# One hybrid decoder layer in f32: w_o's weight sums moved to DRAM, the first pair's norms and rotation placed earlier, the next two pairs' rotation and a table placed later

## The chip, the cores and the metric

The kernel runs on one core of a Trainium2 chip. The metric is the device time of one execution in microseconds (us), lower is better; a time is the median of several executions. The engines that matter are TensorE (PE: matmuls and transposes), VectorE (DVE), ScalarE (ACT), GpSimd (POOL, which here issues some DMAs and raises small vectors to the power -1/2) and the DMA queues that SyncE (SP) and POOL issue. Each engine works through its own list of instructions in order, and an instruction waits until what it reads is there.

## What is computed

One layer on 512 rows of width 2048. The reference, cut to what matters:

```python
h = rms_norm(x, g_mix); z = h @ w_in                       # 2048 -> 7168 columns
aq, ak, av, rq, rk, rv, rg = jnp.split(z, split_at, axis=-1)
aq = rotate(rms_norm_per_head(aq, q_norm)); ak = rotate(rms_norm_per_head(ak, k_norm))
a_out = moba_attention(aq, ak, av)                         # 8 heads of 128, 512 keys, causal
r = retention_chunkwise(rotate(rq), rotate(rk) / sqrt(128), rv)   # 8 heads
r_out = silu(rg) * (rms_norm_per_head(r) * g_ret)
x = x + concat(a_out, r_out) @ w_o                         # 2048 x 2048
h2 = rms_norm(x, g_ffn)
x = x + (silu(h2 @ w_gate) * (h2 @ w_up)) @ w_down         # width 5632
x = x + (p @ w_ple_proj) * sigmoid(rms_norm(x, g_ple) @ w_ple_gate + b)
```

With 512 keys and blocks of 256 the block selection always takes the one past block, so the attention is plain causal attention.

## The kernel before, in words

**Products.** Every f32 product is made of three fast ones. `split` makes of a value a high part (ACT, line 54, `wh` for weights) and a low part (DVE, line 55, `wl` = raw minus `wh`); `mm3` then runs three matmuls on PE (line 63). A weight tile `raw` (128 x 1024, 512 KB) is loaded by SP, split by ACT and DVE, and used by PE. The big projections ("groups") go further: a seven-product scheme (products named 1, 5, 6, 3, 7, 2, 4) needs sums and differences of quarters of the weight matrix. These are either added by DVE on the fly (line 81, `raw<-raw`), or were added ahead in DRAM by transfers that accumulate: `summed` lists such transfers, `move` (line 157) lets POOL issue the next one behind a given ACT instruction (`lead`). Before the change this is done for three parts of w_gate/w_up, w_down and w_ple_gate.

**Stages.** From 0 to about 364 us the first stage runs: the first pair's q and k projection, then four groups (values, pairs, values, gates) driven by `run`, which steps a counter `i` and calls `beside(i)` for loads and other side work. From about 364 to about 740 us the mix runs: for i = 0 to 3 the attention of the pairs of heads, for i = 4 to 7 the retention. A projection of the following pair is cut into pieces, one piece per "slot"; `tick()` counts the slots, and `at_slot(n, fn)` and the tables ATTEND, RETAIN, V_AT and MIXED say at which slot a piece of the attention is written between the matmuls of the projection. So PE always has projection matmuls around an attention piece, and the order of PE's instructions is fixed by the code (`keep_in_program_order`). The order on DVE, ACT, POOL and SP is chosen by a scheduler from the code's order, the dependencies and hints such as `tc.issue_after`. After the mix come w_o (two groups, n = 0 and 1), the gated layer and the last gate until the end.

**The attention of a pair, for each of four blocks of 128 rows** (b = 0 to 3): `load_block` loads z from DRAM (`zr<-z`, SP) where an earlier stage has stored it; `in_place` rotates it on DVE (lines 833, 831, 81: `m<-zr,rope` x2, `zr<-zr,rope`, `zr<-zr,m`), ACT scales it by its norms; PE transposes it (`tp<-ident,zr`), ACT and DVE split it (`qkH`, `qkL`); PE makes scores (`at<-qkL,qkH`), DVE adds the mask, takes the maximum and scales it (lines 913, 915, 917), ACT takes the exponential (`pt`), DVE divides by the sum (lines 921, 922), PE transposes the weights (`tp<-ident,pt`), they are split into PH and PL, and PE multiplies them with the values v. The blocks of the first pair (i = 0) are loaded and rotated at the end of the first stage, their norms made there from squares on ACT and sums on DVE (line 845); the norms of pairs i = 1 and 2 were made in the first stage (`pairs`); pair i = 3 is rotated straight out of its projection. The rotation tables `rope` are built from `cs` and `sn` at the end of the first stage (lines 775 and 778), the retention's table `ropeT` is scaled at slot 32 with PE transposing `rstd` for it. `p_tiles` hands out PH and PL, and a part of each is zeroed once (line 930).

Of the kernel before, what the change touches and what calls it, by code (L numbers as in the profile page):

```python
# [10 lines left out]
F32 = mybir.dt.float32  # L11
F32R = mybir.dt.float32r
# [21 lines left out]
def layer_kernel(ctx, tc, x, xT, pT, g_mix, wqk, w_vg, qk_norm, g_ret, w_ow, g_ffn,  # L34
# [133 lines left out]
    def run(before=lambda i: None, behind=False):  # L168


        i = -3
        parts = {}
        while i < len(steps) or due:
            now[0] = i
            before(i)
            for n, act in ((2, "extract"), (3, "add"), (0, "multiply")):
                if 0 <= i + n < len(steps):
                    g, p, u = steps[i + n]
                    made = getattr(g, act)(p, u)
# [409 lines left out]
    def values(i):  # L589
# [7 lines left out]
                    vd[i][:, tb, k, nh * T:(nh + 1) * T].bitcast(F32), t.bitcast(F32)))  # L597
        return evacuate(finish)

    def pairs():  # L600
        def finish(th, nh, b, part, _):
            tb = 2 * th + b
            t = part
            if (th, nh) == (0, 0):
                t = ev_tile("o", 4, name="zq")
                nc.scalar.activation(t, part, AF.Copy)
            later(1, lambda: nc.sync.dma_start(zd[1 + nh][tb], t))
            sq = ev_tile("o", 4, name="sq")
            ms = stat.tile([P, 4], F32, name=f"ms{nh}_{tb}", bufs=1)
            for j in range(4):  # L610
                c = slice(j * HD, (j + 1) * HD)
                nc.scalar.activation(sq[:, c], t[:, c], AF.Square, accum_out=ms[:, j:j + 1])
            nc.vector.tensor_scalar(ms, ms, 1.0 / HD, eps1[:, tb:tb + 1], op0=ALU.mult, op1=ALU.add)
            power(ms, ms, 4)
            known[1 + nh][tb] = ms
        return evacuate(finish)

    def gates():
# [12 lines left out]
    def beside(i):  # L631

        if i == 3:
            for t, c in ((ident, ident_c), (gf, g_ffn), (gp, g_ple), (gr, g_ret)):
                nc.sync.dma_start(t, c)
        if -2 <= i < NC // 2 - 2:
            if i == -2:
                first.load(0)
            else:
                first.load(i + 2)  # L640
            chunks[i + 2] = []
            for k in (2 * i + 4, 2 * i + 5):
                if i == -2:
                    first.start(k)
                chunks[i + 2].append(h_chunk(k))
        if 0 <= i - 1 < NC // 2:
            first_factors(i - 1, chunks.pop(i - 1))
        for at, q in ((3, "11"), (7, "12"), (11, "22")):
            if at <= i < at + 4:
                groups[0].load(q, i - at)  # L650
        if 8 <= i < 24:
            b, s = divmod(i - 8, NS)
            t = ev_tile("o", 4, name="xn")
            tc.keep_in_program_order(nc.sync.dma_start(t, x[b * P:(b + 1) * P, s * T:(s + 1) * T]))
            nc.scalar.activation(t, t, AF.Square, accum_out=ssq[0][:, b, s:s + 1])
        elif i == 24:
            rstd_of(ssq[0], rstd[0])

            nc.vector.tensor_tensor(eps1, rstd[0], rstd[0], op=ALU.mult)
            nc.vector.reciprocal(eps1, eps1)  # L660
            nc.vector.tensor_scalar(eps1, eps1, EPS, None, op0=ALU.mult)
        if i >= 56 and i % 4 == 0 and i < 112:
            move(gu_moves.pop(0), lead[0])

    run(beside)
    s_ctx.close()
# [36 lines left out]
    stream = [wqk[i, u] for i in range(1, NPAIR + 2) for u in range(NC // 2)] + [pT] + [w_pp[n] for n in range(NS)]  # L703
    ready = []
    fetched = []

    def fetch(behind=None):
        raw = rawq.tile([P, 2, T], F32, name="raw", tag=tags.pop(0))
# [6 lines left out]
    def weights():  # L715
        while fetched + stream and len(ready) < (3 if len(stream) > NS - 1 else 2):
            if not fetched:
                fetch()
            raw = fetched.pop(0)
            wh = wq.tile([P, 2, T], F32R, name="wh", tag="wh")  # L720
            wl = wq.tile([P, 2, T], F32R, name="wl", tag="wl")
            made = split(wh, wl, raw)
            lead[0] = made[0]
            ready.append((wh, wl))
            if gu_moves and slot[0] > 18 and len(stream) % 2:
                move(gu_moves.pop(0), made[0])
        return ready.pop(0)

    def raw_pair():
# [29 lines left out]
    tab = []  # L759
    tabs = [ap.tile([P, 2, NB, HD], F32, name="rope", tag=tag) for tag in ("rope", "rope2")]  # L760
    cs, sn = (ap.tile([P, NB, HD], F32, name=n, tag="pt", bufs=2) for n in ("cs", "sn"))
    nc.sync.dma_start(cs, rope_c[:, 0])
# [8 lines left out]
        return ins  # L771

    blocks = {}
    for s in range(2):
        nc.vector.tensor_tensor(tabs[0][:, s], cs, gain[:, s:s + 1, :].to_broadcast([P, NB, HD]), op=ALU.mult)
        for u in range(2):
            here, there = slice(u * 64, u * 64 + 64), slice(64 - u * 64, 128 - u * 64)
            nc.vector.tensor_tensor(tabs[1][:, s, :, here], sn[:, :, here],
                                    gain[:, s:s + 1, there].to_broadcast([P, NB, 64]), op=ALU.mult)
    rstd1 = rstd[0]  # L780
    last_load = [load_block(0, b) for b in range(NB)][-1]
    for _ in range(4):
# [2 lines left out]
    def load_ropeT():  # L785
        t = ap.tile([P, 2, T], F32, name="ropeT", tag="rope")
        nc.sync.dma_start(t, ropeT_c)
        bc = ev_tile("A", name="bc")
        nc.scalar.activation(bc, over_partitions(rstd1), AF.Copy)
        nc.vector.tensor_tensor(t, t, bc[:, None, :].to_broadcast([P, 2, T]), op=ALU.mult)  # L790
        tab.append(t)

    def qk_pair():
        H = ap.tile([P, T], F32R, name="qkH", tag="qkH", bufs=4)
        L = far.tile([P, T], F32R, name="qkL", tag="qkL", bufs=4)
        return H, L

    def v_of(i):
        v = ap.tile([P, NB, 2, 256], F32R, name="v", tag="v")
        j = i % NPAIR  # L800
        for b in range(NB):
            nc.sync.dma_start(v[:, b].bitcast(F32), vd[i // NPAIR][:, b, :, j * 256:(j + 1) * 256].bitcast(F32))
        return v
# [4 lines left out]
        PL = far.tile([P, 1664], F32R, name="PL", tag="PL")  # L808
        return PH, PL

    kept_p = []

    def weighted(v, ps, j):

# [42 lines left out]

    def in_place(i, b, made, norms):
        of = blocks[i][b]
        sq = squares(of) if i == 0 else None  # L860
        m = rm_tile("m", (P, 2, 2, 2, HD // 2))
        z = of.rearrange("p (s h d) -> p s h d", s=2, h=2)
        whole, *halves = turn(z, m, of, b)
        for step in halves + [whole]:
            step()
        norms.append(norm(b, sq) if i == 0 else known[i][b])
        made.append(rotated(z, m, norms[b]))

    def qk_attn(i):

        made, norms = [], []
        if i == 0:
            for b in range(NB):
                in_place(0, b, made, norms)
        elif i < NPAIR - 1:
            for b in range(NB):
                n = (5, 17)[i - 1] + 2 * b
                at_slot(n, lambda b=b: load_block(i, b, lead[0]))
                at_slot(n + 3, lambda b=b: in_place(i, b, made, norms))
        else:  # L880
# [13 lines left out]
    def attend(z, norms, v, j):  # L894
# [29 lines left out]

        def weights_turned(qb):
            if not ps:
                if not kept_p:
                    kept_p.extend(p_tiles())
                    for t in kept_p:
                        nc.vector.tensor_scalar(t[:, 1408:1536], ident, 0.0, None, op0=ALU.mult)  # L930
                ps.extend(kept_p)
            PH, PL = ps
            nk = (qb + 1) * P
# [20 lines left out]
    def qk_ret(i):  # L954

        made = []
        accs = projection(False)
        both = raw_pair()
        half = HD // 2
        cs, sn = tab[0][:, 0, :], tab[0][:, 1, :]  # L960
# [83 lines left out]
    def mixed(i, made):  # L1044
        spilled = spill(s_mix, i, 0, (lambda shape: rm_tile("o", shape, F32R)) if i < 2 * NPAIR - 2 else None)
        direct = into(s_o, i)
        assert (not s_o) == (i < 2 * NPAIR - 2)
        factors(*made, lambda p: (direct if p in s_o else spilled)(p))

    four = lambda n, m=None: (n, n + 1, *((n + 4, n + 5) if m is None else (m, m + 1)))  # L1050
    V_AT = (3, 27, 54, 80, 100, 119, 144, 162)
# [3 lines left out]
              ((73, four(77), four(81), 89), (83, four(87), four(91), 99)))  # L1055
    RETAIN = (((100, 100, 103, 109, 116), (108, 110, 111, 117, 123)),
# [3 lines left out]
    MIXED = (28, 56, 81, 104, 126, 151, 171, 191)  # L1060

    def heads(i, made):

# [26 lines left out]

    for i in range(2 * NPAIR):
        if i == NPAIR:
            load_ropeT()
        qk = qk_attn(i) if i < NPAIR else qk_ret(i)
        heads(i, qk)
    assert not gu_moves
    h_ctx.close()
    pools["s"] = ctx.enter_context(pool("s2"))
    s_o.update({p: Factors(p) for p in "1563"})
# [52 lines left out]
    for n in range(2):  # L1152
# [4 lines left out]
                            reload(s_c, s_h2, 4, behind | {"1": 4}) if n else lambda p: None))  # L1157

    def swiglu(j):
        kg = min(j // 4, 2)  # L1160
# [207 lines left out]
```

## Time and profile before

| | us |
|---|---|
| median of 3 executions | 2336.1 (2335.06 to 2339.81) |
| the profiled execution, its own time | 2336.76 |
| span of the profiled execution (first to last recorded work) | 2335.0 |
| PE busy within the span | 2296.6 |
| DVE busy | 1926.5 |
| ACT busy | 1229.3 |
| POOL busy | 117.2 |
| moved by DMA | 519.72 MB |

Times in rows of the trace are counted from the start of the span. A row of the timeline has the start, the duration, the engine, the line, the operation, output and inputs, and in brackets the idle time of the engine before it and what released it. A row of the windows has, for each engine, its busy time in the window and the number of its instructions, then the clock that was granted to PE (1.00 is full), the mean busy share of the 16 DMA engines, and GB/s. A row of the waits has the engine and what it was about to do, the engine and the result it waited for, the us in total, how often, and the longest.

### The profile page before, as it was taken

What the parts mean: (1) busy time and instruction counts of PE and PEld (TensorE: products, weight loads), DVE (VectorE), ACT (ScalarE), POOL (GpSimd) and SP (SyncE); (2) the same over time, 40 slices, a digit from 0 to 9 for tenths busy, and PEclk for the clock granted to TensorE, in tenths of its full rate; (3) what the DMA queues carried; (4) which work ended last, traced back from release to release, by engine and by line L of the source; (5) the groups of instructions that cost most, each with busy time, mean ns of one, the idle gap of its engine ahead of it and who ended that gap; (6) DMA issues with size and microseconds to landing.
All of it is one profiled execution on the core that took longest, in us unless ns stands there. A gap on an engine that the chain in (4) does not pass through costs nothing.

```text
span 2335.0 us, 29426 instructions
## 1 busy us (share of the span) xinstructions
PE 2296.6 (98%) x10445; PEld 1891.6 (81%) x10445; DVE 1926.5 (83%) x2601; ACT 1229.3 (53%) x1882; POOL 117.2 (5%) x135
## 2 busy tenths in 40 slices
PE   9999998999999999999999999999999999999999
PEld 7888877788887887888888888888888878888877
DVE  8887777877777987888988898889888877788798
ACT  8646444555565566545554555455445443447643
POOL 0004010100111000000000000000000000000000
PEclk9999999999999999999999999999999999999999
DMA  6635854557686789467556754775596776869863
GB/s 240 233 133 174 268 181 142 167 148 221 188 286 234 285 299 355 139 217 251 160 152 221 251 155 154 224 242 152 188 382 206 253 289 202 295 230 359 293 207 126
DMA packets 183843, 519.72 MB, mean 223 GB/s; under 512 B 20240, under 2 KB 33168, under 8 KB 179600
## 3 DMA queue, kind: packets, MB, share of 16 engines
q1 hardware_dynamic: 169600, 467.50, 56.2%
q0 software_dynamic: 13952, 50.34, 10.1%
q8 instruction: 82, 1.34, 0.2%
q14 instruction: 65, 0.53, 0.1%
q10 hardware_dynamic: 144, 0.01, 0.0%
HBM read 413.95 MB, written 149.95 MB: 242 GB/s over the span
## 4 chain that ended last, share of the span: by engine, by line
PE 53%; DVE 5%; DMA 3%; issue 1%; ACT 1%; SPq 0%; ACTq 0%; DVEq 0%
PE Y L63 23%; PE Z L63 15%; PE X L63 14%; DMA raw<-in_w_dn 2%; DVE wl L55 2%; DVE raw L81 2%; PE tp L68 1%; ACT wh L54 1%; DMA raw<-in_w_gu 0%; DMA pp<-pp 0%; DMA xin<-x 0%; DVE o L55 0%; DVE e L81 0%; DVE t L78 0%; DVE e L1273 0%
## 5 line engine op out<-in xcount | busy, mean ns | idle before, releaser
L54 ACT ACTIVATE wh<-raw 128x1024 fp32r<-128x1024 f32 (+1 forms) x740 | 782.8, 1059 | 867.2 <-PE Y L63 309.5
L55 DVE TENSOR_TENSOR wl<-raw,wh 128x1024 fp32r<-128x1024 f32 (+1 forms) x740 | 902.2, 1222 | 281.9 <-ACT wh L54 280.5
L63 PE MATMUL Y<-wh,s 128*128 128x512 f32 (+1 forms) x1704 | 537.5, 389 | 1.0 <-ACT wh L54 1.0
L81 DVE TENSOR_TENSOR raw<-raw 128x1024 f32<-128x1024 f32 x348 | 420.9, 1223 | 27.9 <-DMA raw<-in_w_vg 11.2
L63 PE MATMUL Z<-wh,s 128*128 128x512 f32 x1212 | 382.3, 389 | 0.2 <-ACT wh L54 0.2
L63 PEld LDWEIGHTS Y<-wh,s 128*128 128x128 f32 x1704 | 319.3, 188 | 66.6 <-ACT wh L54 1.4
L63 PE MATMUL Y<-wl,s 128*128 128x512 f32 x852 | 333.2, 391 | 0.8 <-DVE wl L55 0.4
L63 PE MATMUL X<-wh,s 128*128 128x512 f32 x1008 | 319.2, 390 | 3.8 <-ACT wh L54 2.1
L63 PEld LDWEIGHTS Z<-wh,s 128*128 128x128 f32 x1212 | 227.0, 188 | 46.6 <-ACT wh L54 0.7
L63 PE MATMUL Z<-wl,s 128*128 128x512 f32 (+1 forms) x606 | 238.5, 394 | 2.4 <-DVE wl L55 2.3
L63 PEld LDWEIGHTS X<-wh,s 128*128 128x128 f32 x1008 | 189.1, 188 | 43.8 <-ACT wh L54 2.5
L63 PE MATMUL X<-wl,s 128*128 128x512 f32 x504 | 197.2, 391 | 1.0 <-DVE wl L55 1.0
L63 PEld LDWEIGHTS Y<-wl,s 128*128 128x128 f32 x852 | 160.0, 188 | 36.0 <-DVE wl L55 3.3
L63 PE MATMUL Y<-wh,r 128*128 128x512 f32 x520 | 170.9, 390 | 1.3 <-ACT wh L54 1.3
L63 PE MATMUL acc<-h,wh 128*128 128x512 f32 x512 | 161.4, 396 | 0.0
L63 PEld LDWEIGHTS Z<-wl,s 128*128 128x128 f32 x606 | 113.8, 188 | 27.9 <-DVE wl L55 5.2
L63 PE MATMUL Z<-wh,r 128*128 128x512 f32 x372 | 121.9, 388 | 0.0
L63 PEld LDWEIGHTS Y<-wh,r 128*128 128x128 f32 x520 | 97.4, 188 | 22.0 <-ACT wh L54 2.2
L63 PEld LDWEIGHTS X<-wl,s 128*128 128x128 f32 x504 | 94.6, 188 | 21.6 <-DVE wl L55 2.4
L63 PEld LDWEIGHTS acc<-h,wh 128*128 128x128 f32 x512 | 91.4, 189 | 15.3 <-DVE zr L965 0.2
L63 PE MATMUL Y<-wl,r 128*128 128x512 f32 x260 | 102.3, 394 | 0.5 <-DVE wl L55 0.5
L63 PE MATMUL acc<-h,wl 128*128 128x512 f32 x256 | 100.3, 392 | 0.0
(241 smaller groups left out, 2834.7 us busy)
## 6 DMA issues: line engine op xcount, KB each, us to landing
raw<-in_w_gu SPq DMA_DIRECT2D x172, 512.0 KB, 5.8
raw<-in_w_dn SPq DMA_DIRECT2D x85, 512.0 KB, 6.2
a<-o SPq DMA_DIRECT2D x154, 256.0 KB, 4.9
raw<-in_w_vg SPq DMA_DIRECT2D x64, 512.0 KB, 5.2
s<-a SPq DMA_DIRECT2D x21, 1536.0 KB, 8.6
raw<-in_wqk SPq DMA_DIRECT2D x47, 512.0 KB, 4.8
raw<-in_w_ow SPq DMA_DIRECT2D x32, 512.0 KB, 7.1
xin<-x SPq DMA_DIRECT2D x60, 256.0 KB, 5.9
```

What stands on the lines that cost most here:

```text
L54: return (nc.scalar.activation(H, src, AF.Copy), nc.vector.tensor_tensor(L, src, H.bitcast(F32), op=ALU.subtract))
L55: nc.vector.tensor_tensor(L, src, H.bitcast(F32), op=ALU.subtract))
L63: ins = nc.tensor.matmul(*args, **kw)
L68: ins = nc.tensor.transpose(o, a, ident)
L81: nc.vector.tensor_tensor(o, a, b, op=ALU.add)
```

## The change

Seven edits in one. (1) The sums for the first group of w_o are made in DRAM: 32 more transfers are issued by POOL, in front of the 32 for w_gate/w_up; in the first stage 27 transfers are issued in place of 14, in the mix 37 in place of 18, from slot 9 on with each weight tile; the group then loads ready sums, and DVE's adds for it go. (2) The first pair's squares and norms are made amid the first stage, at i = 42, 46, 50 and 54, from blocks that are loaded once more for it (`zn`, four transfers of 256 KB). (3) The building of the rotation tables and the first pair's rotation are queued on DVE behind given weight splits. (4) v moves to another pool, `qkL` takes its place; PH and PL are handed out and zeroed before the attention begins. (5) Pairs i = 1 and 2 are loaded from slots 4, 8, 12, 16 and 35, 37, 39, 41 in place of 5, 7, 9, 11 and 17, 19, 21, 23, and rotated three slots later. (6) `ropeT` is loaded and scaled at slot 50. (7) The factors of i = 6 are queued behind the last weight split, and two entries of RETAIN and MIXED are one smaller.

```diff
@@ the sums and the first stage
+    s_wo, wo_moves = summed("swo", lambda kh, nh, u: w_ow[0, kh, nh, u], range(4))
     s_gu, gu_moves = summed("sgu", lambda kh, nh, u: w_gu[0, kh, nh, u], range(4))
+    wo_moves += gu_moves
...
+    def squares_of(t, ms, tb):
+        sq = ev_tile("o", 4, name="sq")
+        for j in range(4):
+            c = slice(j * HD, (j + 1) * HD)
+            nc.scalar.activation(sq[:, c], t[:, c], AF.Square, accum_out=ms[:, j:j + 1])
+        nc.vector.tensor_scalar(ms, ms, 1.0 / HD, eps1[:, tb:tb + 1], op0=ALU.mult, op1=ALU.add)
+        power(ms, ms, 4)
...
-        if i >= 56 and i % 4 == 0 and i < 112:
-            move(gu_moves.pop(0), lead[0])
+        if i >= 36 and i % 3 == 0 and i < 117:
+            move(wo_moves.pop(0), lead[0])
+        if i in (42, 46, 50, 54):
+            b = (i - 42) // 4
+            t = ev_tile("o", 4, name="zn")
+            nc.sync.dma_start(t, zd[0][b])
+            known[0][b] = stat.tile([P, 4], F32, name=f"msz_{b}", bufs=1)
+            squares_of(t, known[0][b], b)
@@ the mix: transfers with the weight tiles
-            if gu_moves and slot[0] > 18 and len(stream) % 2:
-                move(gu_moves.pop(0), made[0])
+            if wo_moves and slot[0] > 8:
+                move(wo_moves.pop(0), made[0])
@@ rotation tables, pools
+    queued = ExitStack()
+    queued.enter_context(tc.issue_after(splits[-8][1].ins))
     for s in range(2):
...
+    queued.close()
...
-        L = far.tile([P, T], F32R, name="qkL", tag="qkL", bufs=4)
+        L = ap.tile([P, T], F32R, name="qkL", tag="qkL", bufs=4)
...
-        v = ap.tile([P, NB, 2, 256], F32R, name="v", tag="v")
+        v = far.tile([P, NB, 2, 256], F32R, name="v", tag="v")
...
-    kept_p = []
+    kept_p = p_tiles()
+    for t in kept_p:
+        nc.vector.tensor_scalar(t[:, 1408:1536], ident, 0.0, None, op0=ALU.mult)
@@ rotation of the pairs
-        sq = squares(of) if i == 0 else None
...
-        norms.append(norm(b, sq) if i == 0 else known[i][b])
+        norms.append(known[i][b])
...
-                in_place(0, b, made, norms)
+                with tc.issue_after(splits[b - 6][1].ins):
+                    in_place(0, b, made, norms)
...
-                n = (5, 17)[i - 1] + 2 * b
+                n = (4 + 4 * b, 35 + 2 * b)[i - 1]
                 at_slot(n, lambda b=b: load_block(i, b, lead[0]))
                 at_slot(n + 3, lambda b=b: in_place(i, b, made, norms))
@@ factors of i = 6, tables
+        with ExitStack() as queued:
+            for ins in parted_last if i == 2 * NPAIR - 2 else ():
+                queued.enter_context(tc.issue_after(ins.ins))
+            factors(*made, lambda p: (direct if p in s_o else spilled)(p))
...
-            load_ropeT()
+            at_slot(50, load_ropeT)
@@ w_o
+                            sums=None if n else s_wo))
```

The rows below are instructions in the order in which an engine runs them: line, operation, output and inputs, size, and x and a count for equal ones in a row.

DVE at the end of the first stage, before: the norms' sums and small scalings (`ms`, lines 845 and 846) and the two tables (`rope`) stand around three weight splits.

```order
L55 TENSOR_TENSOR wl<-raw,wh 128x1024
L845 TENSOR_REDUCE ms<-sq 128x4 x3
L757 TENSOR_SCALAR sides<-sides 128x128
L845 TENSOR_REDUCE ms<-sq 128x4
L775 TENSOR_TENSOR rope<-cs,sides 128x512
L846 TENSOR_SCALAR ms<-ms,eps_198 128x4
L778 TENSOR_TENSOR rope<-sn,sides 128x4x64 x2
L846 TENSOR_SCALAR ms<-ms,eps_198 128x4 x2
L775 TENSOR_TENSOR rope<-cs,sides 128x512
L55 TENSOR_TENSOR wl<-raw,wh 128x1024
```

The same place now (the lines are those of the changed kernel):

```order
L55 TENSOR_TENSOR wl<-raw,wh 128x1024
L771 TENSOR_SCALAR sides<-sides 128x128
L791 TENSOR_TENSOR rope<-cs,sides 128x512 x2
L55 TENSOR_TENSOR wl<-raw,wh 128x1024
L794 TENSOR_TENSOR rope<-sn,sides 128x4x64 x4
L55 TENSOR_TENSOR wl<-raw,wh 128x1024
```

Between the first and the second split only `sides` and the two products with `cs` are left.

DVE at the first attention piece of the mix, before: between the two halves of the split of q and k (`qkL`) stands the zeroing of PH and PL.

```order
L55 TENSOR_TENSOR qkL<-tp,qkH 128x512
L930 TENSOR_SCALAR PH<-ident 128x128
L930 TENSOR_SCALAR PL<-ident 128x128
L55 TENSOR_TENSOR qkL<-tp,qkH 128x512
L913 TENSOR_TENSOR at<-at,sides 128x128
```

The same place now:

```order
L55 TENSOR_TENSOR qkL<-tp,qkH 128x512
L852 TENSOR_TENSOR m<-zr,rope 128x4x64 x2
L850 TENSOR_TENSOR zr<-zr,rope 128x512
L55 TENSOR_TENSOR qkL<-tp,qkH 128x512
L830 TENSOR_SCALAR PH<-ident 128x128
L830 TENSOR_SCALAR PL<-ident 128x128
L81 TENSOR_TENSOR zr<-zr,m 128x512
L932 TENSOR_TENSOR at<-at,sides 128x128
```

The zeroing stands behind both halves, and the first block of the second pair (i = 1) is rotated between them.

ACT amid the first stage, now (`zn` are the blocks of the first pair, loaded for their squares; before, only the `wh` and `e` rows stood here):

```order
L54 ACTIVATE wh<-raw 128x1024
L608 ACTIVATE sq,msz_1458<-zn 128x128
L54 ACTIVATE wh<-raw 128x1024
L608 ACTIVATE sq,msz_1458<-zn 128x128 x3
L393 ACTIVATE e_1451<-X_1335 128x512
L54 ACTIVATE wh<-raw 128x1024
L393 ACTIVATE e_1452<-X_1336 128x512
L608 ACTIVATE sq,msz_1542<-zn 128x128 x4
L608 ACTIVATE sq,msz_1624<-zn 128x128 x2
L54 ACTIVATE wh<-raw 128x1024
```

The squares of the first three blocks stand among the weight splits of the pairs group, each behind its load.

More of the change, by code (lines that the diff above doesn't have):

```diff
@@ L159, in layer_kernel @@
     now = [0]
+    splits = []
     lead = [None]
@@ L181, in run @@
                         parts[i + n] = made
+                        splits.append(made)
             with ExitStack() as queued:
@@ L607, in finish @@
             later(1, lambda: nc.sync.dma_start(zd[1 + nh][tb], t))
[L608 to L615, printed above, removed]
+            known[1 + nh][tb] = stat.tile([P, 4], F32, name=f"ms{nh}_{tb}", bufs=1)
+            squares_of(t, known[1 + nh][tb], tb)
         return evacuate(finish)
@@ L705, in layer_kernel @@
     fetched = []
+    parted_last = []
     def fetch(behind=None):
@@ L723, in weights @@
             lead[0] = made[0]
+            parted_last[:] = made
             ready.append((wh, wl))
-            if gu_moves and slot[0] > 18 and len(stream) % 2:
-                move(gu_moves.pop(0), made[0])
+            if wo_moves and slot[0] > 8:
+                move(wo_moves.pop(0), made[0])
         return ready.pop(0)
@@ L758, in layer_kernel @@
     nc.sync.dma_start(mask, mask_c)
-    tab = []
+    tables = []
     tabs = [ap.tile([P, 2, NB, HD], F32, name="rope", tag=tag) for tag in ("rope", "rope2")]
@@ L790, in load_ropeT @@
         nc.vector.tensor_tensor(t, t, bc[:, None, :].to_broadcast([P, 2, T]), op=ALU.mult)
-        tab.append(t)
+        tables.append(t)
     def qk_pair():
         H = ap.tile([P, T], F32R, name="qkH", tag="qkH", bufs=4)
-        L = far.tile([P, T], F32R, name="qkL", tag="qkL", bufs=4)
+        L = ap.tile([P, T], F32R, name="qkL", tag="qkL", bufs=4)
         return H, L
     def v_of(i):
-        v = ap.tile([P, NB, 2, 256], F32R, name="v", tag="v")
+        v = far.tile([P, NB, 2, 256], F32R, name="v", tag="v")
         j = i % NPAIR
@@ L926, in weights_turned @@
             if not ps:
[L927 to L930, printed above, removed]
                 ps.extend(kept_p)
@@ L957, in qk_ret @@
         accs = projection(False)
-        both = raw_pair()
+        both, tab = raw_pair(), tables[0]
         half = HD // 2
-        cs, sn = tab[0][:, 0, :], tab[0][:, 1, :]
+        cs, sn = tab[:, 0, :], tab[:, 1, :]
         for f, acc in enumerate(accs):
@@ L1047, in mixed @@
         assert (not s_o) == (i < 2 * NPAIR - 2)
-        factors(*made, lambda p: (direct if p in s_o else spilled)(p))
+        with ExitStack() as queued:
+            for ins in parted_last if i == 2 * NPAIR - 2 else ():
+                queued.enter_context(tc.issue_after(ins.ins))
+            factors(*made, lambda p: (direct if p in s_o else spilled)(p))
     four = lambda n, m=None: (n, n + 1, *((n + 4, n + 5) if m is None else (m, m + 1)))
@@ L1057, in layer_kernel @@
               ((118, 118, 121, 127, 134), (126, 128, 136, 142, 148)),
[1 row of a table removed]
[1 row of a table added]
               ((161, 168, 171, 177, 184), (161, 178, 179, 185, 191)))
-    MIXED = (28, 56, 81, 104, 126, 151, 171, 191)
+    MIXED = (28, 56, 81, 104, 126, 151, 170, 191)
     def heads(i, made):
@@ L1092, in layer_kernel @@
         if i == NPAIR:
-            load_ropeT()
+            at_slot(50, load_ropeT)
         qk = qk_attn(i) if i < NPAIR else qk_ret(i)
         heads(i, qk)
-    assert not gu_moves
+    assert not wo_moves, len(wo_moves)
     h_ctx.close()
@@ L1156, in layer_kernel @@
                             None if n else in_units(((0, 1, 2), (3,))),
-                            reload(s_c, s_h2, 4, behind | {"1": 4}) if n else lambda p: None))
+                            reload(s_c, s_h2, 4, behind | {"1": 4}) if n else lambda p: None,
+                            sums=None if n else s_wo))
     def swiglu(j):
```

2 rows, old and new, of the table RETAIN are left out of this document.

## The prediction, made before the changed kernel was run

> **What bounds the kernel now.** I read the busy times and the chain that ended last first.
>
> ```profile
> PE 2296.6 (98%) x10445; PEld 1891.6 (81%) x10445; DVE 1926.5 (83%) x2601; ACT 1229.3 (53%) x1882; POOL 117.2 (5%) x135
> PE 53%; DVE 5%; DMA 3%; issue 1%; ACT 1%; SPq 0%; ACTq 0%; DVEq 0%
> ```
>
> PE works for 2296.6 of 2335.0 us, so only 38.4 us of idle time can be won. The change takes no matmul away; it moves a few transposes. Its 20 fewer DVE instructions and 12 more on ACT matter only where PE waits for those engines. What PE waits for:
>
> ```profile
> PE tp L68 <- DVE pt L922: 6.3, 5, 2.9
> PE X L63 <- DVE wl L55: 3.4, 4, 1.8
> PE acc L63 <- ACT pp L1117: 2.2, 1, 2.2
> PE X L63 <- ACT wh L54: 2.1, 1, 2.1
> PE tp L68 <- DVE mx L917: 1.9, 2, 1.4
> PE X L63 <- ACT pp L1117: 1.7, 2, 1.5
> PE at L63 <- DVE pt L995: 1.5, 2, 1.0
> ```
>
> These waits are short, and most lie in the mix. The windows of 10 us from the end of the first stage on show a second cost:
>
> ```profile
> 340.00:350.00 10.00, 8.19 (x35) 6.49 (x34) 9.12 (x20) 6.49 (x10) 3.41 (x3) 0.97 0.92 316
> 350.00:360.00 10.00, 10.00 (x39) 8.07 (x39) 10.00 (x17) 4.30 (x5) 1.95 (x2) 0.86 0.89 287
> 380.00:390.00 10.00, 6.00 (x30) 4.37 (x28) 10.00 (x24) 5.11 (x12) 0.00 (x0) 1.00 0.42 141
> 390.00:400.00 10.00, 9.64 (x42) 7.97 (x43) 6.52 (x18) 4.39 (x11) 0.00 (x0) 0.83 0.18 52
> 410.00:420.00 10.00, 8.27 (x37) 6.19 (x36) 9.92 (x22) 5.91 (x15) 0.87 (x1) 0.83 0.63 160
> 430.00:440.00 10.00, 7.55 (x39) 5.89 (x38) 9.65 (x26) 6.39 (x14) 0.81 (x1) 1.00 0.95 278
> 450.00:460.00 10.00, 10.00 (x53) 8.48 (x52) 3.91 (x12) 4.99 (x14) 1.58 (x2) 1.00 0.43 132
> ```
>
> After the engine columns come PE's granted clock, the DMA share and GB/s. Where PE idles, DVE is full (9.1 to 10.0 of 10 us). And behind three of the gaps the clock falls: 340 to 360 loses (0.03 + 0.14) x 10 = 1.7 us, 390 to 400 and 410 to 420 lose 0.17 x 10 = 1.7 us each. So a gap there costs its length and, by luck of where it falls, 1.7 us more. The gap of 430 to 440 costs no clock.
>
> The Trainium skill, page "TensorE: Matmul & The Clock Gate", section "HAM oscillation — how this bites in real kernels", has as its abstract rule that only idle gaps of PE above about 3.4 us bring the clock down. The trace differs: no wait for DVE is above 2.9 us, and three gaps from 1.7 us up are followed by clocks of 0.83 to 0.86. By the rule the clock would stay whatever these gaps do, and the sum below would be 3.4 us smaller, 2329.8 us, inside the forecast's own range.
>
> **The change part by part.** Savings are made against the profiled execution's own 2336.76 us (span 2335.0 and 1.76 around it), which is 0.66 above the median of 2336.1.
>
> *First rotation, early norms.* The first gap:
>
> ```profile
> 342.11 1.87 DVE L845 TENSOR_REDUCE ms<-sq 128x4 f32<-128x512 f32 x3
> 345.68 0.69 DVE L775 TENSOR_TENSOR rope<-cs,sides 128x512 f32<-128x512 f32 x1 [0.77 <-DMA cs<-in_rope_c]
> 347.95 1.21 DVE L55 TENSOR_TENSOR wl<-raw,wh 128x1024 fp32r<-128x1024 f32 x1
> 349.22 0.66 PE L63 MATMUL X<-wl,h 128*128 128x512 f32 x1 [1.81 <-DVE wl L55]
> ```
>
> The split that PE waits for starts at 347.95. DVE had been held up by norms and tables. In the new order only `sides` and two products with `cs` stand ahead of it. They still need the load of `cs`, here to 345.68. Two products of 0.69 us end about 347.0, so the split is 0.95 us earlier: gap 0.86 us. Bounds: 0 (the load comes later by as much) and 1.81. A gap of 0.86 should also spare the clock: 1.7 us. Term: 2.65 us.
>
> The norms return in the first stage. One block's squares cost what the pairs' squares cost there:
>
> ```profile
> 174.85 0.31 ACT L612 ACTIVATE sq<-v 128x128 f32<-128x128 f32 x1 [0.58 <-DVE v L81]
> 145.89 0.50 PE L63 MATMUL Z<-wl,s 128*128 128x512 f32 x1 [0.43 <-DVE wl L55]
> 100.00:150.00 50.00, 49.57 (x219) 40.74 (x218) 44.99 (x50) 26.54 (x31) 1.01 (x1) 1.00 0.58 210
> ```
>
> Four squares with their read-outs are about 1.2 us for a block (0.3 us from one start to the next), 4.8 us in all; ACT is busy 26.5 of 50 us there, so the work itself fits. But three of the four blocks stand in a row between 138 and 150 us among the splits, each behind its load, and there DVE is busy 45 of 50 us, with PE at 145.89 already waiting. I charge 0.7 us. Bounds: 0 and 4 us (two loads that are late by one block's 1.2 us each, and one lost clock stretch of 1.7).
>
> *Zeroing of PH and PL.*
>
> ```profile
> 369.56 0.23 DVE L930 TENSOR_SCALAR PH<-ident 128x128 fp32r<-128x128 f32 x1 [2.07 <-DMA sg<-e]
> 371.47 0.39 PE L63 MATMUL at<-qkL,qkH 128*128 128x256 f32 x1 [1.49 <-DVE qkL L55]
> zr<-z SPq DMA_DIRECT2D x12, 256.0 KB, 2.9
> ```
>
> DVE stood 2.07 us between the halves of `qkL`, because PH and PL sit where a store was still reading. Now they stand behind both halves. But the first rotation of pair 1 stands between them instead and waits for its load: about 365.7 (when the split that lets SP issue it is done) + 2.9 = 368.6, then three DVE operations of together 1.5 us, then the split: 370.1 in place of 370.73. I take 1.0 of the 1.49 us. Bounds: all 1.49, and a loss of 2.1 if the load takes 3 us more.
>
> *Pairs 1 and 2.* DVE is full because four blocks of pair 1 come together with the scores of pair 0:
>
> ```profile
> 378.87 1.43 DVE L833 TENSOR_TENSOR m<-zr,rope 128x256 f32<-128x256 f32 x4 [0.82 <-DMA zr<-z]
> 385.39 0.63 PE L68 MATMUL tp<-ident,zr 128*128 128x128 f32 x4 [1.40 <-DVE mx L917]
> 390.36 0.87 PE L68 MATMUL tp<-ident,pt 128*128 128x128 f32 x3 [2.95 <-DVE pt L922]
> ```
>
> A block costs DVE 1.43/2 + 0.69 + 0.65, about 2 us. With one block every four slots, one of the four comes before 376 and one after 402, which takes 4 us out of the full stretch of 379 to 392. Each block now waits for its own load in DVE's queue, up to 1 us as in the 0.82 of the row, and the scores' `mx` and `pt` are queued behind it. Of 1.40 + 2.95 = 4.35 us I take 2.0 away and leave 2.35 in three pieces, each too short for the clock: 1.7 us more. Bounds: 0 and 4.35 + 1.7.
>
> ```profile
> 411.88 0.52 PE L68 MATMUL tp<-ident,pt 128*128 128x128 f32 x3 [0.48 <-DVE mx L917]
> 413.64 0.66 PE L68 MATMUL tp<-ident,zr 128*128 128x128 f32 x4 [1.25 <-DVE qkL L55]
> ```
>
> Here pair 2 was rotated (8 us of DVE between 406 and 419), which now comes at 440 to 460, where the windows show DVE at 3.9 of 10 us from 450 on. 0.48 + 1.25 = 1.73 us go, and the clock's 1.7 with them: 3.4 us. Bounds: 1.7 and 3.4.
>
> *The table at slot 50.*
>
> ```profile
> 436.38 0.60 PE L68 MATMUL tp<-ident,rstd 128*128 128x128 f32 x4
> 439.22 0.63 PE L68 MATMUL tp<-ident,pt 128*128 128x128 f32 x4 [2.25 <-DVE pt L922]
> ```
>
> The four transposes of `rstd` filled time in which PE would wait for `pt` anyway. DVE's list ahead of that `pt` is the same as before, and the table's own DVE work stood behind it. So PE waits 0.4 us longer here and does the transposes elsewhere: a loss of 0.4. A gap of 2.65 us is as long as others that cost the clock, and I charge 1.7. Bounds of this part: a loss of 2.1 and a gain of 0.5.
>
> *w_o's sums.* This row stands for DVE between 685 and 900 us:
>
> ```profile
> L81 DVE TENSOR_TENSOR raw<-raw 128x1024 f32<-128x1024 f32 x32 | 38.8, 1223 | 0.4 <-DMA raw<-in_w_ow 0.2
> ```
>
> Half of these, 16 x 1.22 = 19.6 us, go. PE's waits there that DVE ends are the two for `pt` of line 995 (1.5 us); I take 1.5, and 0.9 for short waits for weight splits. The waits for ACT (`pp` 2.2 and 1.7, `wh` 2.1) I leave: the `pp` copies keep their place behind the same ACT instructions. Bounds: 0 and 2.4 + 6.0. The price is 32 more transfers:
>
> ```profile
> q0 software_dynamic: 13952, 50.34, 10.1%
> DVE raw L81 <- DMA raw<-in_w_vg: 8.3, 5, 3.2
> sgu<-in_w_gu POOLq DMA_DIRECT2D x13, 512.0 KB, 6.2
> ```
>
> The 88 transfers of before and 4 MB for `pp` took 10.1% of 2335 us, 236 us for 50.34 MB. One of 0.524 MB so holds all 16 DMA engines for 2.46 us; 32 more are 79 us, spread over 570 us. The last two rows are of the stretch 190 to 340 us: DVE waits 8.3 us for weight loads there, beside 13 transfers, and PE hardly at all (DVE has that much in hand). I cost them at nothing. If that cover is gone, each costs up to 8.3/13 = 0.64 us, the third rival below.
>
> Sum: 2.65 - 0.7 + 1.0 + 3.7 + 3.4 - 2.1 + 2.4 = 10.4 us; 2336.76 - 10.4 = 2326.4, about 2326 against the median of 2336.1, 0.4% faster.
>
> **The rivals.**
>
> *The waits are only replaced (chance 0.22).* For: each block of pair 1 now waits for a load on DVE's in-order queue, and those loads are issued only when a weight split on ACT is done, which itself stands behind scalings that wait for DVE. Then the gaps of 349, 371 and 385 to 390 stay with two clock losses, and left are 3.4 from pair 2, 2.4 from w_o, -0.7 and -0.4: 4.7 us, 2332. Against: the DVE order does put the splits first.
>
> *More goes than I count (0.13).* The three ACT waits are partly ACT behind DVE. If 2.1 + 2.2 + 1.5 go too, no clock is lost at 439 (1.7) and pair 1's remaining 2.35 us vanish, it is 10.4 + 9.9 = 20.3 us: 2316.5. Against: the ACT order round the `pp` copies is unchanged.
>
> *Slower: the transfers reach PE (0.07).* One mechanism: weight loads queue behind POOL's doubled transfers. At 0.64 us each, 32 transfers cost 20.5 us; with every gain above the end is 2346.9. It decides once the loads are late by more than DVE's lead, that is, when PE sees more than 15.1 of the 20.5 us.
>
> ```profile
> 680.00:700.00 20.00, 17.83 (x83) 14.69 (x82) 15.76 (x32) 14.72 (x31) 6.56 (x11) 1.00 1.03 385
> ```
>
> For: here the DMA engines are full already. Against: elsewhere the windows shown have shares of 0.18 to 0.95, and PE does not wait for `raw` in its list at all. The Trainium skill, page "DMA: Bandwidth & Descriptors", section "Issuing engines are not separate DMA queues", says that DMAs issued from different engines run interleaved on the same 16 DMA engines, which speaks for this rival; no run here shows how they share them, and the chance rests on the rows alone.
>
> That the change does not do what it says: the scheduler might keep the rotation where it was. The order of the engines shows it moved, so this has no chance of its own.
>
> **How the numbers follow.** Forecast 0.58 (2321 to 2331 by its bounds, as not all fall to one side), rivals 0.22, 0.13 and 0.07. A measurement of this kernel tells 0.2%, 4.7 us, from no change (the runs shown differ by 4.75), so faster is below 2331.4. Nearly all of the forecast (0.55), the second rival and 0.09 of the first are faster: 0.77; 0.16 within; slower 0.07. The range goes from 2315, the second rival with its tail, to 2338, where the first rival's loads take the longer bound and the third rival sets in.
>
> **What would show it.** In the changed profile: the gap at about 349 below 1 us with PE's clock at 1.00 behind it; DVE never idle between the halves of `qkL` for a store; no wait at the place of 413.64; pair 1's stretch with under 2.5 us of idle; the gap at 439 longer by 0.4; no `raw<-raw` for the first w_o group and no wait for line 995. The forecast is wrong if loads of `zn` or `zr` stand as releasers before weight splits, or if clock losses appear in the first stage.

## The result, and the profile after

The changed kernel is slower: median 2351.04 us of 4 runs (2347.65 to 2353.62) against 2337.78 us of 4 runs of the kernel before, a ratio of 1.0057 with a 95% interval of 1.0038 to 1.0075. The profiled execution took 2347.65 us, its span is 2345.9 us. The prediction was 2326 us, so not even the sign was right.

The first row is PE's in the busy times of the changed kernel, the others are what PE waits for there (line numbers of the changed kernel).

```profile
PE 2302.0 (98%) x10445; PEld 1895.6 (81%) x10445; DVE 1908.2 (81%) x2581; ACT 1232.5 (53%) x1910; POOL 147.4 (6%) x167
...
PE tp L68 <- DVE pt L941: 7.3, 6, 5.6
PE Z L63 <- DVE wl L55: 4.6, 7, 2.2
PE Y L63 <- DVE wl L55: 4.5, 3, 3.1
PE X L63 <- ACT wh L54: 3.9, 2, 3.6
```

PE's idle time (span less busy) grew from 38.4 to 43.9 us, its busy time by 5.4 us for the same matmuls. DVE did lose 18 us of work, and PE waits for DVE all the same, in other places. Some of the windows of 10 us show where:

```profile
170.00:180.00 10.00, 6.86 (x31) 5.34 (x30) 5.54 (x7) 2.66 (x6) 0.00 (x0) 1.00 0.62 163
180.00:190.00 10.00, 10.00 (x39) 8.08 (x38) 5.92 (x10) 7.12 (x26) 3.89 (x4) 0.83 0.99 289
250.00:260.00 10.00, 9.03 (x33) 7.29 (x34) 7.93 (x8) 2.13 (x2) 0.38 (x1) 0.83 0.73 194
...
350.00:360.00 10.00, 8.81 (x39) 6.97 (x38) 6.30 (x14) 4.27 (x5) 0.52 (x1) 1.00 0.85 316
390.00:400.00 10.00, 8.51 (x45) 6.66 (x45) 8.07 (x19) 4.09 (x9) 0.52 (x1) 1.00 0.42 120
410.00:420.00 10.00, 9.14 (x49) 7.46 (x48) 5.89 (x14) 4.43 (x9) 0.83 (x1) 1.00 0.79 163
430.00:440.00 10.00, 6.70 (x30) 4.90 (x29) 7.15 (x19) 4.71 (x10) 0.82 (x1) 0.99 1.04 323
440.00:450.00 10.00, 7.51 (x27) 6.24 (x28) 9.79 (x21) 2.14 (x3) 1.73 (x2) 0.67 0.39 111
700.00:710.00 10.00, 7.82 (x31) 6.36 (x30) 6.81 (x16) 6.83 (x14) 2.54 (x5) 0.83 1.04 402
890.00:900.00 10.00, 9.78 (x39) 7.76 (x38) 8.17 (x11) 5.46 (x10) 1.01 (x1) 0.83 1.03 420
2280.00:2290.00 10.00, 10.00 (x39) 8.10 (x39) 8.78 (x8) 4.87 (x6) 0.00 (x0) 0.85 0.13 43
```

The three losses of clock at 350 to 360, 390 to 400 and 410 to 420 are gone. New are losses behind gaps at 179 us and at 442 us (this one is 3.4 us in all: 0.01 x 10 and 0.33 x 10), with four more of 1.7 us behind 250, 705, 889 and 2278 us. Added over all windows of 10 us in which PE works, the lost clock is 5.1 us before and 11.9 us after. Of the 3.4 us at 442, 1.4 us fall into the gap itself, where PE does nothing: its clock is 0.50 from 439.7 us on. What is left, 10.5 less 5.1 us, is the 5.4 us by which PE's busy time grew. So the growth of the span by 10.9 us is half idle time and half lost clock.

The places of equal instructions show how it builds up. The split of the first gap of before (PE at 349.22) stands at 356.58 now: the first stage lost 7.4 us, against a gain that was forecast. The transposes of 439.22 stand at 442.49, so the mix up to there won 4.1 us, its own wait of 5.59 us included. The projection matmul that waited at 698.53 stands at 705.02, 6.5 us late; of the 3.2 us that this is more than at 442, 2.0 are the slow clock behind that gap.

Why the first stage lost time, in rows of the changed kernel from POOL, DVE and PE (start, duration, instruction, and in brackets the idle time and its releaser):

```profile
160.59 0.86 POOL L157 DMA_DIRECT2D swo<-in_w_ow  x1 [4.49 <-ACT wh L54]
168.81 0.85 POOL L157 DMA_DIRECT2D swo<-in_w_ow  x1 [7.36 <-ACT wh L54]
...
176.46 1.23 DVE L81 TENSOR_TENSOR raw<-raw 128x1024 f32<-128x1024 f32 x1 [4.46 <-DMA raw<-in_w_vg]
178.88 0.50 PE L63 MATMUL Y<-wl,s 128*128 128x512 f32 x1 [3.14 <-DVE wl L55]
...
248.56 1.23 DVE L81 TENSOR_TENSOR raw<-raw 128x1024 f32<-128x1024 f32 x1 [4.59 <-DMA raw<-in_w_vg]
250.97 0.50 PE L63 MATMUL Z<-wl,s 128*128 128x512 f32 x1 [2.17 <-DVE wl L55]
```

DVE waits for a weight load, and its split comes late to PE. The time from issue to landing of the `raw` loads between 158 and 182 us (minimum, median, maximum), first before, where POOL issues no transfer in this stretch, then after, points to the cause:

```profile
DMA to landing us min/median/max: 3.4/3.7/4.7
```

```profile
DMA to landing us min/median/max: 3.4/5.0/6.9
```

A load is issued when a weight buffer comes free, that is, just in time. The 1.3 us more in the median are not made up, since each late load frees its buffer late for the next: SP issues nine of these loads in the stretch before and seven after. The kernels of the experiments below fall on the same two sides. With the changed kernel's transfers there the median is 4.5 us (e1), 4.6 (e3) and 4.8 (e5), without them 3.6 (e2 and e4).

In the mix it is stores that come late. These are rows of ACT and PE at the pair that is rotated straight out of its projection:

```profile
434.99 0.60 ACT L859 ACTIVATE sq<-acc 128x512 f32<-128x512 f32 x1 [2.29 <-DMA mix<-o]
438.21 0.60 ACT L859 ACTIVATE sq<-acc 128x512 f32<-128x512 f32 x1 [2.62 <-DMA mix<-o]
...
442.49 1.09 PE L68 MATMUL tp<-ident,pt 128*128 128x128 f32 x4 [5.59 <-DVE pt L941]
```

ACT's squares wait until stores of `mix` have freed their buffers, the exponential and DVE's rotation stand behind them, and PE waits 5.59 us for the weights of the last block.

### The profile page after: what moved, and what is told of

Same layout as the page of the kernel before. It is cut to its first block, busy times and chain, and to the rows that moved or that the text cites. A ratio compares the mean times of both kernels' runs of the same rounds, so it can differ in the third digit from the quotient of the medians.

```text
span 2345.9 us, 29537 instructions
## 1 busy us (share of the span) xinstructions
PE 2302.0 (98%) x10445; PEld 1895.6 (81%) x10445; DVE 1908.2 (81%) x2581; ACT 1232.5 (53%) x1910; POOL 147.4 (6%) x167
## 4 chain that ended last, share of the span: by engine, by line
PE 78%; DVE 9%; DMA 8%; issue 2%; ACT 2%; SPq 0%; POOL 0%; ACTq 0%; DVEq 0%; POOLq 0%
PE Y L63 30%; PE Z L63 20%; PE X L63 17%; PE acc L63 8%; DVE wl L55 3%; DVE raw L81 3%; PE at L63 2%; DMA raw<-in_w_dn 2%; PE tp L68 2%; DMA raw<-in_w_vg 1%; ACT wh L54 1%; DMA mix<-o 1%; DMA h<-o 1%; DMA raw<-in_w_gu 0%; DMA v<-v 0%
## 5 line engine op out<-in xcount | busy, mean ns | idle before, releaser
L81 DVE TENSOR_TENSOR raw<-raw 128x1024 f32<-128x1024 f32 x332 | 400.8, 1220 | 31.5 <-DMA raw<-in_w_vg 17.8
```

The source lines that it names most:

```text
L81: nc.vector.tensor_tensor(o, a, b, op=ALU.add)
```

## The experiments

Theory T, from these rows: the 32 more transfers of POOL hold up loads and stores that come just in time. Rival N: the early norms with their loads are the cost. Rival P: the new pools and the later rotation are. All ratios are to the kernel before on the same chip; its runs there had medians of 2339 to 2342 us.

**Edit 1 alone (e1), all but edit 1 (e2).** e1 is the kernel before with

```diff
+    s_wo, wo_moves = summed("swo", lambda kh, nh, u: w_ow[0, kh, nh, u], range(4))
+    wo_moves += gu_moves
-        if i >= 56 and i % 4 == 0 and i < 112:
-            move(gu_moves.pop(0), lead[0])
+        if i >= 36 and i % 3 == 0 and i < 117:
+            move(wo_moves.pop(0), lead[0])
-            if gu_moves and slot[0] > 18 and len(stream) % 2:
-                move(gu_moves.pop(0), made[0])
+            if wo_moves and slot[0] > 8:
+                move(wo_moves.pop(0), made[0])
+                            sums=None if n else s_wo))
```

and e2 is the changed kernel with these lines as they were before.

> The kernel before with edit 1 alone: w_o's sums in DRAM, the 32 more transfers and their new places. Theory T (the transfers that POOL issues hold up the weight loads): slower than before by 6 to 10 us, about 2346 us, with PE waits above 1.5 us for weight splits between 170 and 260 us, where DVE waits for raw loads. Theory N (the early norms with their extra loads are the cost) and theory P (the new pools and the later rotation are the cost): 2 us faster than before, about 2336 us, with none of these waits.

> The changed kernel without edit 1: transfers and adds on DVE as before, all else changed. T: faster than before by 3 to 8 us, about 2332 us, no PE wait above 1 us between 150 and 300 us, and the wait at about 440 us back to some 2.5 us. N and P: still slower than before, 2345 us or more.

Measured: e1 1.0067 (1.0043 to 1.0091), median 2356.9 us; e2 0.9972 (0.9958 to 0.9987), median 2336.4 us. So edit 1 is the cause of the loss, and N and P fall: edit 1 costs 16 us on the old kernel, and without it the other edits win 6.5 us. e1's size was missed, 16 in place of 6 to 10 us. e2's rows of PE at the places of the prediction:

```profile
349.69 0.50 PE L63 MATMUL X<-wl,h 128*128 128x512 f32 x1 [0.69 <-DVE wl L55]
384.04 0.63 PE L68 MATMUL tp<-ident,zr 128*128 128x128 f32 x4 [0.84 <-DVE sm L938]
386.55 0.52 PE L68 MATMUL tp<-ident,pt 128*128 128x128 f32 x3 [0.50 <-DVE pt L939]
388.81 0.63 PE L68 MATMUL tp<-ident,pt 128*128 128x128 f32 x4 [0.35 <-DVE pt L939]
395.23 0.50 PE L63 MATMUL at<-PH,v 128*128 128x512 f32 x1 [0.92 <-ACT pt L937]
408.89 0.66 PE L68 MATMUL tp<-ident,zr 128*128 128x128 f32 x4 [0.86 <-DVE qkL L55]
432.63 0.63 PE L68 MATMUL tp<-ident,pt 128*128 128x128 f32 x4 [2.58 <-DVE pt L939]
```

Pair 1's stretch keeps 0.84 + 0.50 + 0.35 + 0.92 = 2.61 us of the 4.35, in pieces, and the only lost clock of e2 is the 1.7 us behind 432.63.

**The norms where they were (e3), the transfers elsewhere (e4).** e3 takes the zn loads and their squares out of the first stage and makes squares and norms in `in_place` again. e4 has

```diff
-        if i >= 36 and i % 3 == 0 and i < 117:
+        if 34 <= i <= 44 or 61 <= i <= 64 or 89 <= i <= 100:
```

> The changed kernel without edit 2: the first pair's norms made where they were before, no zn loads. T: within 3 us of the changed kernel, 2348 to 2354 us. N: 2342 us or less. P: as T.

> The changed kernel with the first stage's 27 transfers put where SP issues no weight loads in the trace of before (steps 34 to 44, 61 to 64 and 89 to 100 of the first stage in place of every third step from 36 to 114). T: the waits at 178.9 and 251.0 us go, 5 to 8 us faster than the changed kernel, about 2344 us. N and P: no change, 2351 us.

Measured: e3 1.0050 (1.0033 to 1.0067), as the changed kernel, so N falls here too. e4 1.0027 (1.0016 to 1.0037): 0.3% or 7 us better than the changed kernel by moving transfers alone, and the waits at 179 and 251 us are gone. A new wait of 2.34 us for a weight split on ACT stands at 147.9 us, where the transfers of steps 34 to 44 meet the squares, which wait for `zn` loads. The wait for the weights of the last block stays as long as it was, 5.55 us, now at 439 us.

**More transfers without their use (e5, e6).** Both are e2 with sums of w_o made in DRAM that nobody reads; DVE's adds stay. e6 only adds transfers; e5 adds 13 and also gives the 14 that were there the places of the changed kernel.

```diff
 e5:
+            move((wo_moves if i < 75 else gu_moves).pop(0), lead[0])
 e6:
             if gu_moves and slot[0] > 18 and len(stream) % 2:
                 move(gu_moves.pop(0), made[0])
+            elif slot[0] > 8 and wo_moves:
+                move(wo_moves.pop(0), made[0])
```

(e5 with the changed kernel's condition on i.)

> The kernel of e2 (all edits but w_o's sums) with 13 transfers more in the first stage alone, at the places of the changed kernel; their sums are made and read by nobody, and w_o's adds stay on DVE. Theory T1 (a transfer of POOL costs time where it meets a weight load that comes just in time, and that is the first stage above all): 7 us slower than e2, within 2 us of before, with PE waits of 2 to 3 us at about 179 and 251 us. Theory T2 (the mix and the DMA engines' sheer load are the cost): within 2 us of e2, 6 us faster than before.

> The kernel of e2 with 22 transfers more in the mix alone (one at each weight tile from slot 9 on), read by nobody. T1: 3 to 5 us slower than e2, most of it at about 435 us, where ACT waits for stores of mix and PE for the weights of a block some 5 us; nothing in the first stage. T2: 10 us or more slower than e2.

Measured: e5 1.0007 (0.9994 to 1.0020), 0.35% or 8 us above e2, as T1 had it. Its wait at 179.61 us is 3.45 us, but the one at 251 is only 0.53, and one of 2.77 us for a weight split stands at 356.81 us. In the profiles the same split of weights, at 349.69 us in e2, comes 7.1 us later in e5 and 6.9 us later in the changed kernel: e5 has the changed kernel's loss in the first stage whole. e6 1.0004 (0.9989 to 1.0018), 0.32% or 7.5 us above e2, more than T1's 3 to 5 us and less than T2's 10. And its place was missed: the wait at 433 is only 3.10 us, and the loss lies at 690 to 720. Rows of e6: what ACT waits for between 690 and 716 us, then PE:

```profile
ACT pp L1136 <- DMA mix<-o: 5.9, 2, 5.5
...
713.91 0.79 PE L63 MATMUL X<-wh,s 128*128 128x512 f32 x1 [4.43 <-ACT pp L1136]
```

In e2 that stretch has a wait of 2.56 us at its place. So transfers cost time at the end of the mix, where the windows from 670 to 710 us show a DMA share of 1.02 to 1.04 in e2 already. But this is not the changed kernel's loss: e6 issues transfers until 695 us, the changed kernel until 677, and at the place of 713.91 the changed kernel waits only 1.30 us. Its own loss in the mix, 3.0 us against e2 in the profiles, lies at the wait of 5.59 us at 442, and what makes that one so long stays open. e6 has a transfer with each weight tile before it as well and waits 3.10 us, and e4 has lost the waits of the first stage and still waits 5.55.

**All edits with 64 transfers in places taken for quiet (e7), the rotation early again (e8).** e7 is e3 with 38 transfers at steps 15 to 22, 34 to 45, 60 to 64 and 89 to 101 and 26 in the mix. e8 is e2 with

```diff
-                n = (4 + 4 * b, 35 + 2 * b)[i - 1]
+                n = (5, 17)[i - 1] + 2 * b
```

> All edits but the early norms, with w_o's sums in DRAM, and the 64 transfers put where no weight loads are due: 38 in the first stage (steps 15 to 22, 34 to 45, 60 to 64, 89 to 101), 26 in the mix, none between slots 23 and 35. T1: all transfers are there and cost next to nothing, so the time is that of e2 less up to 1.5 us for DVE's adds: 6 to 8 us faster than before. T2: as many bytes as in the changed kernel, so 6 us or more slower than before.

> The kernel of e2 with the next two pairs' rotation at its old slots (5 to 11 and 17 to 23). If the later rotation took its gaps as the prediction had it (2.0 and 1.7 us idle, 1.7 us of clock each): 5 to 7 us slower than e2, about the time of before, with PE waits of 3 us at 385 us and of 1.7 us at 410 us. Rival: the early norms and the freed queue of DVE did it, and this kernel is within 2 us of e2.

Measured: e7 1.0052 (1.0033 to 1.0070), a clear miss for the expectation of T1. Rows of e7's PE and ACT:

```profile
95.11 0.80 PE L63 MATMUL Z<-wl,s 128*128 128x512 f32 x1 [3.90 <-DVE wl L55]
...
213.87 1.06 ACT L54 ACTIVATE wh<-raw 128x1024 fp32r<-128x1024 f32 x1 [4.85 <-DMA raw<-in_w_vg]
222.03 0.49 PE L63 MATMUL X<-wh,h 128*128 128x512 f32 x1 [3.00 <-ACT wh L54]
```

Two of the four places were not quiet: steps 15 to 22 run into the loads of 84 us and after, steps 60 to 64 into the last loads of their group, which SP still issues at 205 us. Steps 34 to 45 and 89 to 101 have no wait beyond those of before. In the profiles e7 is 17.5 us behind e2, 11.2 of them by the end of the first stage; of the later waits, those at 446, 722 and 893 us are longer than e2's at these places. So the miss fits collisions as the mechanism, but it does not show that all 64 transfers can be hidden; no run does.

e8: 1.0013 (1.0002 to 1.0024), 0.41% or 9.6 us slower than e2 (expected: 5 to 7; its profiled execution was its fastest, only 1.0 us above e2's), with waits of 2.94 us at 388.5 and 1.25 us at 411.5 us and lost clock at both again. The later rotation is the part of the change that wins; without it the others gain nothing that shows.

**Placing the transfers better (e9 to e12).** e9 is e2 with

```diff
-        if i >= 56 and i % 4 == 0 and i < 112:
+        if 89 <= i <= 99:
             move(gu_moves.pop(0), lead[0])
-            if gu_moves and slot[0] > 18 and len(stream) % 2:
+            if gu_moves and slot[0] > 36:
                 move(gu_moves.pop(0), made[0])
```

e10 is e9 with `load_ropeT()` at slot 32 again. e11 is e2 with e5's 13 unread transfers at steps 89 to 101. e12 is the kernel before with e9's two lines and nothing else.

> The kernel of e2 with its 32 transfers put elsewhere: 11 in the first stage at steps 89 to 99, where no weight load is due, none before, and 21 in the mix from slot 37 on, one at each weight tile, none in the last 30 slots. T1: the waits for weight splits that e2 keeps at 326 us (1.18) go, the wait at 432 us is 2.6 us or less, the wait for pp at 708 us (2.56) shrinks: 2 to 5 us faster than e2, 8 to 11 us faster than before. If only the number of transfers counts: the time of e2.

> The kernel of e9 with edit 6 undone: the retention table is loaded and scaled at slot 32 again. As the prediction costs edit 6 (0.4 us of PE work no longer hidden, and a longer gap at about 432 us that then costs 1.7 us of clock): 0.5 to 2.5 us faster than e9. Otherwise within noise of it.

> The kernel of e2 with the same 13 transfers more in the first stage as in e5, read by nobody, but at steps 89 to 101, where no weight load is due. T1: within 2 us of e2, 5 us or more faster than before, and no PE wait over 1 us for a weight split between 150 and 300 us. If it is their number or the bytes: 7 us slower than e2, as e5.

> The kernel before with nothing changed but the places of its 32 transfers, as in e9 (11 at steps 89 to 99 of the first stage, 21 from slot 37 on). T1: the 14 transfers of before's first stage cost little on PE (its waits for weight splits at 299 and 325 us are 0.97 us in all), so 1 to 5 us faster than before, and the mix's gaps at 385 to 390, 413 and 439 us stay. If e9's gain over e2 comes from the other edits: the time of before.

Measured: e9 0.9953 (0.9935 to 0.9971), median 2328.9 us: the best of all, 11 us faster than before, as expected, and 4.4 us than e2, though the intervals of e9 and e2 overlap. The waits that the expectation names behave as it says: none above 0.7 us at 326, 2.50 us at 429, 1.04 us for `pp` at 704. e12 0.9985 (0.9973 to 0.9997): the places alone win about 3.5 us on the old kernel, and its gaps at 386, 409 and 436 us stay, as expected. e10 0.9955 (0.9938 to 0.9971): edit 6 makes no difference that can be told.

e11 0.9993 (0.9978 to 1.0009): 0.21% above e2 where at most 0.1% was expected, and 0.14% below e5. Its interval overlaps that of e2 a little and that of e5 more, so this is half a support. Its profile has no PE wait over 0.76 us in the stretch of the added transfers (270 to 320 us). A wait of 2.31 us stands at 249.20, ahead of them, where e11 and e2 issue the same transfers. First DVE of e2, then DVE and PE of e11:

```profile
245.17 1.23 DVE L81 TENSOR_TENSOR raw<-raw 128x1024 f32<-128x1024 f32 x1 [2.64 <-DMA raw<-in_w_vg]
```

```profile
246.78 1.23 DVE L81 TENSOR_TENSOR raw<-raw 128x1024 f32<-128x1024 f32 x1 [3.98 <-DMA raw<-in_w_vg]
249.20 0.50 PE L63 MATMUL Z<-wl,r 128*128 128x512 f32 x1 [2.31 <-DVE wl L55]
```

Two loads come late there in a row. In e2 DVE waits 0.37 us at 239.57 for the one ahead and then these 2.64, 3.01 us together, and PE waits 0.23 us for the split behind them. In e11 DVE waits 1.11 and 3.98, 5.09 us together, and PE 2.31. Both differences are 2.78 us: that much DVE has in hand at this place, and 14 transfers in the first stage use it up already. How much of e11's 5 us this wait makes in the mean of its runs stays open, since only one was profiled.

Number and place both count in these runs. Among the kernels with the later rotation, 32 transfers give 0.9953 (e9) and 0.9972 (e2), 45 give 0.9993 (e11) and 1.0007 (e5), 54 give 1.0004 (e6), and 64 give 1.0027 (e4), 1.0050 (e3), 1.0052 (e7) and 1.0057 (the changed kernel). At one number the place moves the time by 0.14 to 0.30%. Clear of the intervals are only e4 against the changed kernel and, just so, e12 against before. That a transfer which meets no load costs nothing is not shown.

## Why the prediction was wrong, by its own steps

**The step that failed: the 32 transfers "I cost them at nothing".** Edit 1, which brings them, costs about 20 us (the changed kernel against e2, 1.0057 to 0.9972; by their intervals 14 to 25), and 16 us on the old kernel (e1), both with its gain on DVE taken off. The two profiled executions lie 11.5 us apart: 6.9 arose in the first stage, where e5 shows the transfers as the cause, 3.0 at the wait of 442 us, and the rest behind the mix. What is missing to 20 us lies between executions of which no trace was kept. The sign that the prediction itself named came true, lost clock in the first stage.

The third rival, with a chance of 0.07, had the mechanism for the weight loads right. That its sum of 20.5 us fits is in part luck: it took its 0.64 us per transfer from waits of DVE and not of PE, e5 gives 8/13 = 0.62 but e6 only 7.5/22 = 0.34, and the late stores of the mix are not in it.

Two readings led to the term of nothing. First, "PE hardly at all (DVE has that much in hand)" took an absence of long waits for a reserve. The trace of before shows that it was spent. Behind the longest of DVE's five waits, 3.22 us, PE already waits:

```profile
322.39 1.23 DVE L81 TENSOR_TENSOR raw<-raw 128x1024 f32<-128x1024 f32 x1 [3.22 <-DMA raw<-in_w_vg]
...
324.81 0.50 PE L63 MATMUL Z<-wl,r 128*128 128x512 f32 x1 [0.54 <-DVE wl L55]
```

The difference, 2.68 us, is close to the 2.78 us of e2 and e11. Second, 79 us of transfers were held against the DMA share averaged over 570 us, while loads collide in single stretches of 10 us.

The other terms, one by one:

- **The first gap** was right: 0.86 us predicted, 0.69 in e2 and 1.19 in the changed kernel, no lost clock. **The early norms** were charged 0.7 us; e3 takes away both their cost and their gain, and its time is the changed kernel's within the intervals, so it does not price the term by itself; but PE's matmul of 250.97 us stands at 250.80 in e3, so up to there no cost of the squares and their loads above 0.2 us shows.
- **Zeroing of PH and PL:** the wait for `qkL` is gone, but e2 has a new one of 0.94 us just ahead (PE for DVE's `e`), so at most 0.55 of 1.49 us are won, 1.0 predicted.
- **Pairs 1 and 2:** 2.35 us left of pair 1's 4.35 predicted, 2.61 in e2; 1.73 us predicted to vanish at 412, 0.86 left; the clock saved at both. e8 shows the mechanism; its 9.6 us are more than the 7.1 of the sum (3.7 and 3.4).
- **The table at slot 50:** in the profile of e2 as predicted (a wait of 2.58 us in place of 2.25, and 1.7 us of clock), but the times of e9 and e10 agree, so the loss of 2.1 us is not borne out in the time.
- **w_o's adds:** 16 of 32 went, as predicted. Of PE's 1.5 us for `pt` of retention 0.97 stay, the 0.53 for a weight split went; the wait for `wh` at about 890 us grew from 2.07 to 3.57 us. So of 2.4 us at most half came.
- Without the transfers, the terms of the sum make 10.4 - 2.4 = 8 us; e2 has 6.5 us (3.0 to 9.8 by its interval).

## What to carry to other kernels

A wait that does not reach the bounding engine is not a reserve: read how long it is at its longest, against how far the engine behind it is ahead at that place, before adding traffic. Transfers that run in the background cost time where they meet loads and stores that come just in time. The mean DMA share did not tell that price here, and more of them cost more at every placing that was tried. The list of the queue's loads shows the stretches without any. Work that is spread out on an engine that is off the bound (one block every four slots here) pays where that engine is full and the bounding one waits for it.

## What the runs showed of the hardware that was not expected

- Of gaps of the same length on PE some cost 1.7 us of clock and some do not: 2.17 us at 698.53 before left the clock at 1.00, 2.18 us at 705.02 after is followed by 0.83 between 700 and 710. Amid the span the clock falls to 0.50 for 3.41 us or twice that, and within each of the traces all these stretches begin a whole number of 3.41 us apart (before at 349.40, 390.36 and 414.25 us, 12 and 7 of them). Windows on this grid, two of before and two of the changed kernel, show the difference:

```profile
694.15:697.56 3.41, 2.21 (x12) 1.73 (x10) 3.41 (x10) 2.85 (x6) 0.00 (x0) 1.00 1.02 408
697.56:700.97 3.41, 2.44 (x12) 2.09 (x13) 3.41 (x5) 1.99 (x4) 1.08 (x2) 1.00 1.06 393
```

```profile
702.56:705.97 3.41, 1.23 (x7) 0.88 (x6) 3.40 (x8) 3.31 (x6) 0.55 (x2) 1.00 1.05 387
705.97:709.38 3.41, 3.41 (x12) 2.72 (x11) 0.85 (x2) 1.50 (x3) 1.62 (x3) 0.50 1.03 406
```

The gap of before is split over two windows, 1.20 and 0.97 us, and the other lies in one, 2.18 us. In these two traces, from 25 us on, every slow stretch comes behind a window in which PE is idle for at least 1.62 us, and no window with more than 1.71 us of idle time is without one behind it. So where a gap falls on the grid decides, and part of the changed kernel's loss is luck of this kind: the two waits of 1.18 and 0.44 us behind which the clock falls at 2279.5 us stand in before too, at 2268 and 2269 us, and cost no clock there. The clock shows in the spread as well: of the kernel before, beside the experiments, the 14 executions at a mean clock of 0.998 took 2337.1 us on average and the 11 at 0.995 took 2346.6.

- POOL's power of two small vectors (128 x 4) took 17.93 us where DVE was busy without a break, against 1.00 to 2.00 us for a single one elsewhere in the trace, and the transfers behind it in POOL's list left late and two at once, just ahead of a stretch of weight loads. Rows of before:

```profile
198.60 1.00 POOL L84 TENSOR_TENSOR ms<-ms,neghalf 128x4 f32<-128x4 f32 x1 [1.71 <-DVE ms L613]
...
211.41 17.93 POOL L84 TENSOR_TENSOR ms<-ms,neghalf 128x4 f32<-128x4 f32 x2 [6.35 <-DVE ms L613]
229.30 1.47 POOL L157 DMA_DIRECT2D sgu<-in_w_gu  x2
```

The Trainium skill, page "SBUF — State Buffer", section "🔬 SBUF: two separate sides", tells of a port pair that a DVE instruction with two SBUF inputs or a GpSimd instruction holds alone for its whole length. The rows agree with it; no run here took the DVE work away to try it.
